# One stop for a unit's Gram products, its inverse in three parts of five steps, and fewer plain products between the mixers' steps

## The chip, the cores and the metric

The kernel runs on one core of a Trainium2 chip. The time is device microseconds from launch to end. It was 2159.46 us in the median of three runs (2154.07 to 2161.47).

## The reference

One transformer block over 1024 tokens of width 1024, in f32. Three stages add to the residual `x`:

```
x = x + 0.5 * (silu(norm(x) @ w_gate) * (norm(x) @ w_up)) @ w_down     # ffn 1, hidden 2816
proj = norm(x) @ w_in
o_gla  = gla(proj part)      # 4 heads, chunks of 64: decay, scores, state
o_rwkv = rwkv7(proj part)    # 8 heads of 64, token by token:
    sa    = state @ a_t
    state = state * w_t + sa b_t^T + v_t k_t^T
    y_t   = state @ r_t
x = x + concat(o_gla, o_rwkv) @ w_out
x = x + 0.5 * ffn 2(norm(x)) ; out = norm(x)
```

The token-by-token recurrence `rwkv7` is what the change is about. The kernel computes it in chunks of 64 tokens. Within a chunk, the effect of the tokens on one another is a triangular 64x64 system for each head. Its inverse is needed before the chunk's state can be taken on.

## The kernel before

**Halves.** The sequence is cut into two halves of 512 tokens, A and B. Every f32 product of the feed-forward parts and projections runs as three passes over operands split into a high and a low part (`mm3`). These are the *plain products* below: matmuls of 128x512, on TensorE one after the other. Their weights are staged by a cast on ScalarE (`wH`, L459) and a subtraction on VectorE (`wL`, L460), six buffers each.

**Mixers.** `mixers(h, filler, last)` runs once for A (with half B's ffn 1 as filler) and once for B (with half A's ffn 2 as filler). It has four streams:

- `Quad.prep` makes, for each of four units of two chunks (`u` = 0 to 3), the Gram products `pg` (L82 to L87), the 16x16 triangular inverse (L103 to L109: 15 steps of a shuffle, a multiplication and an addition on VectorE), then by small products `p1`, `p1b`, `p2`, `p2b` the 64x64 inverse, and `pav`.
- `Quad.loop` takes the state on, chunk by chunk: `pz`, `pu`, `px`, `py`, each waiting for an eviction of the one before.
- `Quad.norm` normalizes a unit's output: reductions and a Newton square root on VectorE (L226 to L233), four transposes `pyT`, eight scaled copies on ScalarE (L244), two operations on VectorE (L248), a store to DRAM (L249).
- `gla_unit`, twice: `pkv`, `pA`, five levels `pB`, `po`, `pt`.

**What sets TensorE's order.** Each stream yields a latency, `LAT[...]` times `SLACK` (1.49), in an estimated clock `T.ns` that adds up only TensorE's own work. As long as no stream is due, one plain product of the filler is put in. When some are due, those within `NEAR` take their next step, and then the filler gives `int(ns * FILL / 216 + 0.999)` plain products, `ns` being the estimate of what the steps took. TensorE keeps this order; the other engines' orders come from a list scheduler. That scheduler may also draw work from behind the mixers into places where it expects TensorE to be idle: the first `run(f1b, n=3)` after the mixers (two halves of a down product, one unit of gate and up: 96 plain products) lies among the mixers' steps.

**Behind the mixers.** `outprep` loads the mixers' results back from DRAM (`xnL`, L1289) and splits them (`xnH` on ScalarE, L1290; `xnL` on VectorE, L1291). They use memory that the mixers' tiles held. `outproj` multiplies them by `w_out` (`pout`), which needs the last unit's `norm` to have ended. For half B, `to_store(A)` also runs there: eight additions on GpSimd (`xs`, L717), each through one of the five buffers `t2` that the feed-forward's `silu` and `hf` use too, and a store each.

Of the kernel before, what the change touches and what calls it, by code (L numbers as in the profile page):

```python
# [5 lines left out]
CDEC=float(np.exp(-0.5))  # L6
MULT,ADD,SUB,MAX,MIN=ALU.mult,ALU.add,ALU.subtract,ALU.max,ALU.min

LAT=dict(pre=8000,gram=0,c32=3000,inv2=1400,D=900,m1=900,m2=900,x2=700,pav=900,w=600,z=1000,u=1000,x=1500,gn=6000,gpre=2635,gfirst=8000,lev0=5723,lev=1944,sc=770,on=8372)

def const_array():
    p=np.arange(128)
# [35 lines left out]
class Quad:  # L48
# [6 lines left out]
    def prep(self):  # L55
# [8 lines left out]
        for u in range(4):  # L64
# [8 lines left out]
            BK=BK.rearrange("p q (c r)->p q c r",c=2)  # L73
            yield LAT["pre"] if u==0 else 0

            WA=[mt([8,64],"WA","WA") for h in range(2)]
            W=st.W=[mt([8,64],"W","W") for h in range(2)]
            for i in range(2):
                c4=slice(4*i,4*i+4)
                pg=[ps(f"pg{h}").rearrange("p (e x t)->p e x t",e=4,x=2) for h in range(2)]  # L80
                for e in range(4):
                    q,c=2*i+e//2,e%2  # L82
                    for h in range(2):
                        T.matmul(pg[h][:,e],BK[fr[h],q,c],AR[fr[h],q,:,c,:],start=True,stop=True,tile_position=(64*h,0))
                for x,Wx in ((1,WA),(0,W)):
                    for h in range(2):
                        V.tensor_tensor(Wx[h][:,c4],pg[h][:,:,x],mg[:,x:x+1,:].to_broadcast([128,4,64]),op=MULT)  # L87
                yield LAT["gram"]

            c32=mt([8,32],"i2","c32")  # L90
            for h in range(2):
# [9 lines left out]
            V.tensor_copy(R16,C["i16"].rearrange("p (o t)->p o t",o=1).to_broadcast([128,8,16]))  # L101
            yield LAT["c32"]
            for j in range(15):  # L103
                n=15-j
                lb=mt([8,n],"lb","lb",bufs=2,padded_shape=[128,8,16])
                V.stream_shuffle(lb,c16[:,:,j+1:16],[j]*16+[16+j]*16)
                V.tensor_tensor(lb,lb,R16[:,:,j:j+1].to_broadcast([128,8,n]),op=MULT)
                V.tensor_tensor(R16[:,:,j+1:16],R16[:,:,j+1:16],lb,op=ADD)
                if j%2: yield LAT["inv2"]  # L109

            R=mt([8,32],"Rd","R")
            S.mul(R[:,:,0:16],R16,C["mq0"])
# [1 line left out]
            D=mt([8,32],"i2","D")  # L114
            V.transpose(D.rearrange("p c t->p (c t)"),R.rearrange("p c t->p (c t)"))
            yield LAT["D"]
            p1=ps("p1")[:,0:256].rearrange("p (c t)->p c t",t=32)
# [4 lines left out]
            S.copy(X1,p1)  # L122
            yield LAT["m1"]
            p1=ps("p1b")[:,0:128].rearrange("p (c t)->p c t",t=16)
# [4 lines left out]
            D=mt([8,32],"i2","D2")  # L129
# [29 lines left out]
            pav=ps("pav")  # L159
# [194 lines left out]
D = 1024  # L354
# [17 lines left out]
MUIDX = {**{f"r{i}": i for i in range(4)}, **{f"k{i}": 4 + i for i in range(4)}, **{f"v{i}": 8 + i for i in range(4)}, "wa": 12, "g": 13}  # L372
BUFS = dict(s2=7, W=4, WA=2, WN=4, AR=2, UV=2, AV=2, R64=2, s1=2, i2=3, g1=3, s3=2)
SLACK = 1.490
FILL = 0.549
PAHEAD = 2
NEAR = 254.150
NH, NL, NR = 6, 6, 4
# [14 lines left out]
def block_kernel(tc, ctx, x, consts, coff, vecs, finaln, wgu, wdn, win_t, win_v, w_out, alw, wa2, g2, out):  # L393
# [832 lines left out]
    def mixers(h, filler, last):  # L1226
# [40 lines left out]
        with tc.manual_schedule(engines={mybir.EngineType.PE}):  # L1267
            while True:
# [5 lines left out]
                if any(s.at <= t0 for s in can):  # L1274
                    for s in can:
                        if s.at <= T.ns + NEAR:
                            s.step()
                    n = int((T.ns - t0) * FILL / 216.0 + 0.999)
                for _ in range(n):
# [274 lines left out]
```

## Time and profile before

| | |
|---|---|
| profiled execution | 2156.78 us |
| its span, first to last instruction | 2155.0 us |
| median of three runs | 2159.46 us |
| TensorE (PE) busy | 2041.7 us, 95% |
| VectorE (DVE) busy | 1457.4 us, 68% |
| ScalarE (ACT), GpSimd (POOL) busy | 42%, 25% |
| mean granted clock of TensorE | 0.978 |

The profiled execution is 2.7 us under the median of the runs. A busy TensorE row counts pipelined matmuls, so 95% says only that TensorE is seldom idle. The useful question is where the remaining idle time lies and what ends it. The mixers of A run from 760 us, those of B from 1271 us.

### The profile page before, as it was taken

The page shows a single profiled execution, that of the slowest core. Times are in us where ns is not written, and L with a number is a line of the kernel's source. Part 1 is how long each engine was busy: PE and PEld are TensorE (multiplying, and loading weights), DVE is VectorE, ACT ScalarE, POOL GpSimd, SP SyncE. Part 2 cuts the span into 40 slices and gives each one's busy share as a digit, 9 for nine tenths or more (in the row PEclk, how much of TensorE's full clock was granted, in tenths as well). Part 3 has the DMA queues.
Part 4 walks back from the last instruction along what each step waited for, and adds up shares of the span by engine and source line. Part 5 has one row for each costly group of instructions (what it writes and reads, how often), then busy time and mean ns, then how long its engine had stood idle before and what let it go on. Part 6 is the DMA issues. An engine that isn't in the chain of part 4 may idle for free.

```text
span 2155.0 us, 36173 instructions
## 1 busy us (share of the span) xinstructions
PE 2041.7 (95%) x13516; PEld 1632.1 (76%) x13516; DVE 1457.4 (68%) x3043; ACT 909.9 (42%) x1699; POOL 549.3 (25%) x558
## 2 busy tenths in 40 slices
PE   8899999989999999996999999999598999998998
PEld 7777888867788877775788887777476788886886
DVE  6675778747739776775566956766577577874665
ACT  6432344322456545444365644534244243432143
POOL 0411555467012300000001310000112145647610
PEclk9999999999999999998999999999799999999999
DMA  5433344587355763333335683332433333448652
GB/s 192 128 117 112 124 146 166 205 312 270 131 177 187 234 187 110 114 104 134 126 124 181 215 260 123 115 109 80 161 130 106 112 127 132 161 167 341 244 171 74
DMA packets 172639, 345.20 MB, mean 160 GB/s; under 512 B 17296, under 2 KB 56240, under 8 KB 172464
## 3 DMA queue, kind: packets, MB, share of 16 engines
q1 hardware_dynamic: 145312, 251.13, 35.2%
q0 software_dynamic: 23552, 80.76, 10.4%
q10 hardware_dynamic: 3600, 11.01, 1.4%
q8 instruction: 106, 1.74, 0.3%
q14 instruction: 69, 0.57, 0.1%
HBM read 243.21 MB, written 99.61 MB: 159 GB/s over the span
## 4 chain that ended last, share of the span: by engine, by line
PE 81%; DVE 8%; DMA 4%; issue 2%; ACT 2%; POOL 2%; SPq 0%; ACTq 0%; DVEq 0%; POOLq 0%
PE pju L43 21%; PE pgu L43 17%; PE pp L43 11%; PE pdn L43 10%; PE pjd L43 7%; PE pout L43 4%; PE pv L43 2%; PE po L43 1%; PE py L43 1%; DVE wL L460 1%; DVE x L898 1%; DMA hh<-d_hid 1%; DVE T L696 1%; PE ptn L46 1%; PE pt L46 1%
## 5 line engine op out<-in xcount | busy, mean ns | idle before, releaser
L460 DVE TENSOR_TENSOR wL<-raw,wH 128x512 fp32r<-128x512 f32 (+1 forms) x382 | 274.2, 726 | 263.2 <-ACT wH L459 261.5
L459 ACT CAST wH<-raw 128x512 fp32r<-128x512 f32 (+1 forms) x382 | 233.6, 618 | 376.7 <-PE pgu L43 118.8
L43 PE MATMUL pgu<-xnH,wH 128*128 128x512 f32 (+1 forms) x656 | 259.4, 397 | 0.3 <-ACT xnH L518 0.2
L43 PE MATMUL pgu<-xnL,wH 128*128 128x512 f32 (+1 forms) x656 | 258.8, 396 | 0.0
L43 PE MATMUL pgu<-xnH,wL 128*128 128x512 f32 (+1 forms) x656 | 258.4, 395 | 0.0
L43 PE MATMUL pju<-T,wH 128*128 128x512 f32 x768 | 240.7, 394 | 2.4 <-ACT wH L695 2.4
L43 PE MATMUL pjd<-wH,hh 128*128 128x512 f32 x640 | 207.1, 403 | 13.1 <-DMA hh<-d_hid 12.7
L43 PEld LDWEIGHTS pju<-T,wH 128*128 128x128 f32 x768 | 144.3, 188 | 36.7 <-ACT wH L695 3.3
L43 PEld LDWEIGHTS pjd<-wH,hh 128*128 128x128 f32 x640 | 123.7, 193 | 45.0 <-issue 14.3
L43 PE MATMUL pju<-T,wL 128*128 128x512 f32 x384 | 151.4, 394 | 0.0
L43 PEld LDWEIGHTS pgu<-xnH,wH 128*128 128x128 f32 x656 | 124.7, 191 | 28.2 <-ACT xnH L518 1.1
L43 PEld LDWEIGHTS pgu<-xnL,wH 128*128 128x128 f32 x656 | 124.2, 190 | 27.6 <-DVE xnL L519 0.7
L43 PEld LDWEIGHTS pgu<-xnH,wL 128*128 128x128 f32 x656 | 124.0, 189 | 26.7 <-DVE wL L460 0.4
L43 PE MATMUL pdn<-wH,hH 128*128 128x512 f32 x320 | 129.9, 407 | 11.9 <-DVE hf L668 8.3
L43 PE MATMUL pp<-xnH,wH 128*128 128x512 f32 x352 | 140.7, 400 | 0.0
L43 PE MATMUL pp<-xnL,wH 128*128 128x512 f32 x352 | 138.9, 395 | 0.0
L43 PE MATMUL pp<-xnH,wL 128*128 128x512 f32 x352 | 138.9, 395 | 0.0
L43 PE MATMUL pjd<-wL,hh 128*128 128x512 f32 x320 | 129.6, 405 | 6.1 <-DVE wL L696 6.1
L43 PE MATMUL pdn<-wL,hH 128*128 128x512 f32 x320 | 129.3, 404 | 0.8 <-DVE wL L460 0.8
L43 PE MATMUL pdn<-wH,hL 128*128 128x512 f32 x320 | 129.0, 403 | 1.2 <-DVE hL L672 1.2
L696 DVE TENSOR_TENSOR wL<-s,wH 128x512 fp32r<-128x512 f32 x96 | 98.9, 1032 | 29.3 <-ACT wH L695 29.3
L631 DVE SCALAR_TENSOR_TENSOR x<-pdn,x 128x512 f32<-128x512 f32 x144 | 98.5, 686 | 28.9 <-PE pdn L43 27.8
(393 smaller groups left out, 4321.7 us busy)
## 6 DMA issues: line engine op xcount, KB each, us to landing
raw<-in_wgu_dram SPq DMA_DIRECT2D x256, 256.0 KB, 2.6
hh<-d_hid SPq DMA_DIRECT2D x80, 512.0 KB, 4.5
d_hid<-hh POOLq DMA_DIRECT2D x76, 512.0 KB, 3.7
raw<-in_win_t_dram SPq DMA_DIRECT2D x88, 256.0 KB, 3.1
raw<-in_wdn_dram SPq DMA_DIRECT2D x80, 256.0 KB, 2.8
wdk<-in_wdn_dram SPq DMA_DIRECT2D x24, 512.0 KB, 7.5
d_x<-x SPq DMA_DIRECT2D x20, 512.0 KB, 2.6
raw<-in_w_out_dram SPq DMA_DIRECT2D x32, 256.0 KB, 2.7
```

The source lines that it names most:

```text
L43: return self.t.matmul(out,lhsT,rhs,**kw)
L46: return self.t.transpose(out,in_,idn)
L459: S.copy(H, raw)
L460: V.tensor_tensor(L, raw, H.bitcast(F32), op=SUB)
L631: V.scalar_tensor_tensor(h.x[tt][:, co], ps, 0.5, h.x[tt][:, co], op0=MULT, op1=ADD)
L696: V.tensor_tensor(L, f, H.bitcast(F32), op=SUB)
L898: V.scalar_tensor_tensor(x, v, k, x, op0=MULT, op1=ADD)
```

## The change

Nothing is computed otherwise, and every engine has as many instructions of each kind as before (10892 matmuls, for one). What changes is where `prep` stops, with which latencies, and the filler's share.

```
-LAT=dict(pre=8000,gram=0,c32=3000,inv2=1400,D=900,m1=900,m2=900,...
+LAT=dict(pre=8000,gram=1500,c32=1600,inv5=3300,D=900,m1=900,m2=900,...
...
             for i in range(2):
                 ...                                  # 8 pg matmuls, 4 evictions L87
-                yield LAT["gram"]
+            yield LAT["gram"]
...
             for j in range(15):
                 ...                                  # shuffle, multiply, add
-                if j%2: yield LAT["inv2"]
+                if j%5==4: yield LAT["inv5"]
...
-FILL = 0.549
+FILL = 0.3
```

Both groups of Gram products now come at one stop. The inverse has three stops (after steps 5, 10 and 15) where it had seven. After a set of due steps the filler gives about half as many plain products.

TensorE, the end of half A's mixers, from the last state product `py` to the first product of `outproj`. Before:

```order
L43 MATMUL pz<-Xn,AR 64x64 x8
L43 MATMUL pgu<-xnL,wH 128x512
L43 MATMUL pgu<-xnH,wL 128x512
L43 MATMUL pu<-Z,R_9913 64x64 x8
L43 MATMUL px<-UV,WN 64x64 x8
L43 MATMUL py<-Xn,AR 64x64 x2
...
L43 MATMUL py<-UV,W 64x64 x2
L46 MATMUL pyT<-ct,AV 128x128 x4
L43 MATMUL pout_10345<-wH,xnH 128x512
```

And now:

```order
L43 MATMUL py<-UV,W 64x64 x2
L43 MATMUL pdn<-wH,hL 128x512
...
L43 MATMUL pdn<-wH,hL 128x512
L43 MATMUL pgu<-xnH,wH 128x512
...
L43 MATMUL pgu<-xnH,wL 128x512
L46 MATMUL pyT<-ct,AV 128x128 x4
L43 MATMUL pgu<-xnH,wH 128x512
...
L43 MATMUL pgu<-xnH,wL 128x512
L43 MATMUL pout_10345<-wH,xnH 128x512
```

40 `pdn` and 6 `pgu` stand between the last `py` and `pyT`, and 42 `pgu` between `pyT` and `pout`, where there was nothing. Of the 520 plain products that stood between the first `pg` and the last `py` of a mixer, 432 are left there. In half B it is the same.

ScalarE at the same place (`sq` is the square of L230, `wH` a cast of a weight). Before:

```order
L208 COPY AV<-py 128x256
L230 ACTIVATE sq_10092<-AV 128x512
L244 ACTIVATE AV<-pyT,vt 64x128 x8
L1290 CAST xnH<-xnL 128x512 x7
L459 CAST wH<-raw 128x512
```

And now:

```order
L208 COPY AV<-py 128x256
L230 ACTIVATE sq_10092<-AV 128x512
L459 CAST wH<-raw 128x512 x4
L244 ACTIVATE AV<-pyT,vt 64x128 x8
L459 CAST wH<-raw 128x512 x2
L665 ACTIVATE silu<-pgu 128x512
L459 CAST wH<-raw 128x512 x2
L1290 CAST xnH<-xnL 128x512
```

Eight casts of weights and one `silu` have come in between the last `py` and the first `xnH`, four casts and the `silu` of them behind L244.

VectorE there, in the middle of the Newton steps (`nwt`, `nwy`) of the last unit. Before:

```order
L231 TENSOR_REDUCE vr<-sq_10092 128x8
L485 TENSOR_SCALAR nwa<-vr 128x8
L486 TENSOR_SCALAR nwt<-nwa 128x8
L487 TENSOR_SCALAR nwy<-nwt 128x8
L492 TENSOR_TENSOR nwt<-nwy 128x8
L493 TENSOR_TENSOR nwt<-nwt,nwa 128x8
```

And now:

```order
L231 TENSOR_REDUCE vr<-sq_10092 128x8
L631 SCALAR_TENSOR_TENSOR x<-pdn,x 128x512
L485 TENSOR_SCALAR nwa<-vr 128x8
L460 TENSOR_TENSOR wL<-raw,wH 128x512
L486 TENSOR_SCALAR nwt<-nwa 128x8
L631 SCALAR_TENSOR_TENSOR x<-pdn,x 128x512
L487 TENSOR_SCALAR nwy<-nwt 128x8
L460 TENSOR_TENSOR wL<-raw,wH 128x512
L492 TENSOR_TENSOR nwt<-nwy 128x8
L631 SCALAR_TENSOR_TENSOR x<-pdn,x 128x512
L493 TENSOR_TENSOR nwt<-nwt,nwa 128x8
```

Evictions of the `pdn` products and subtractions of weights now stand among the steps of the norm; the last eviction but one stands ahead of the second Newton step's last operation (L494).

## Rows read from the trace of the kernel before

**Rows 1.** The page: busy time by engine, and TensorE in 40 slices

```profile
PE 2041.7 (95%) x13516; PEld 1632.1 (76%) x13516; DVE 1457.4 (68%) x3043; ACT 909.9 (42%) x1699; POOL 549.3 (25%) x558
...
PE   8899999989999999996999999999598999998998
```

**Rows 2.** TensorE's waits within half A's mixers: who, for whom, us, times, longest

```profile
PE pout L43 <- ACT xnH L1290: 9.5, 1, 9.5
PE pyT L46 <- DVE AV L233: 6.8, 1, 6.8
PE pA L43 <- DVE ke L289: 2.3, 2, 1.2
PE p2b L43 <- ACT X L141: 1.2, 2, 0.8
PE px L43 <- DVE UV L192: 1.1, 1, 1.1
```

**Rows 3.** The same within half B's mixers

```profile
PE pout L43 <- ACT xnH L1290: 11.4, 1, 11.4
PE pyT L46 <- DVE AV L233: 10.1, 1, 10.1
...
PE pu L43 <- DVE Z L186: 1.2, 1, 1.2
```

**Rows 4.** Timeline, end of half A's mixers: start us, us, engine, line, operation, tiles

```profile
995.34 0.42 DVE L201 TENSOR_TENSOR Xe<-Xt,pc 128x256 f32<-128x256 f32 x1
...
997.00 0.37 ACT L208 COPY AV<-py 128x256 f32<-128x256 f32 x1 [2.88 <-PE py L43]
...
1003.75 1.09 PE L46 MATMUL pyT<-ct,AV 128*128 128x128 f32 x4 [6.79 <-DVE AV L233]
1004.87 3.72 ACT L244 ACTIVATE AV<-pyT,vt 64x128 f32<-64x128 f32 x8 [5.14 <-PE pyT L46]
...
1009.35 0.69 DVE L248 TENSOR_TENSOR AV<-AV,g 128x512 f32<-128x512 f32 x1
...
1013.69 0.62 ACT L1290 CAST xnH<-xnL 128x512 fp32r<-128x512 f32 x1 [5.10 <-DMA xnL<-d_mix]
```

**Rows 5.** Timeline, end of half B's mixers: GpSimd beside VectorE

```profile
1509.13 1.59 POOL L717 TENSOR_TENSOR xs<-xnH,xnL 128x512 f32<-128x512 f32 x1 [37.40 <-ACT wH L459]
...
1511.64 2.92 DVE L201 TENSOR_TENSOR Xe<-Xt,pc 128x256 f32<-128x256 f32 x1
...
1515.19 2.65 DVE L227 TENSOR_SCALAR sm<-sm 128x8 f32<-128x8 f32 x1
1515.32 2.48 POOL L717 TENSOR_TENSOR xs<-xnH,xnL 128x512 f32<-128x512 f32 x2
```

**Rows 6.** The chain of waits in both halves: start us, us, what

```profile
962.40 7.65 PE pdn L43 x32
970.06 5.82 PE pgu L43 x25
...
1529.67 2.59 DMA d_mix<-AV
```

**Rows 7.** Stretches: us, busy by engine, granted clock of TensorE (PEclk), DMA

```profile
774.80:807.80 33.00, 31.92 (x502) 24.87 (x498) 30.39 (x121) 14.57 (x29) 0.20 (x1) 1.00 0.49 136
...
762.30:997.10 234.80, 228.95 (x3220) 175.26 (x3218) 165.89 (x593) 108.63 (x217) 1.77 (x5) 0.99 0.41 123
...
1014.30:1017.80 3.50, 3.44 (x8) 2.72 (x9) 2.56 (x4) 1.86 (x4) 0.00 (x0) 0.50 1.01 357
...
1390.80:1400.50 9.70, 9.70 (x33) 6.73 (x33) 1.98 (x3) 1.63 (x3) 0.00 (x0) 0.63 0.25 83
1400.50:1403.50 3.00, 3.00 (x8) 2.42 (x8) 1.95 (x6) 0.60 (x1) 0.00 (x0) 0.50 0.00 0
...
1535.80:1540.10 4.30, 4.30 (x10) 3.39 (x11) 2.92 (x5) 2.70 (x5) 0.00 (x0) 0.50 0.97 314
```

More of the change, by code (lines that the diff above doesn't have):

```diff
@@ L7 @@
 MULT,ADD,SUB,MAX,MIN=ALU.mult,ALU.add,ALU.subtract,ALU.max,ALU.min
-LAT=dict(pre=8000,gram=0,c32=3000,inv2=1400,D=900,m1=900,m2=900,x2=700,pav=900,w=600,z=1000,u=1000,x=1500,gn=6000,gpre=2635,gfirst=8000,lev0=5723,lev=1944,sc=770,on=8372)
+LAT=dict(pre=8000,gram=1500,c32=1600,inv5=3300,D=900,m1=900,m2=900,x2=700,pav=900,w=600,z=1000,u=1000,x=1500,gn=6000,gpre=2635,gfirst=8000,lev0=5723,lev=1944,sc=770,on=8372)
 def const_array():
```

## The prediction

> **What bounds the kernel now.** I read the page first. TensorE is busy 95% of the span, and no other engine over 68% [rows 1]; it has the same matmuls before and after. So a gain can only be idle time of TensorE that goes, or time in which it ran at half its clock. The slices show two dips, a 6 and a 5: the ends of the two mixers.
>
> The waits of each mixer then say what ended that idle time. In half A, 16.3 us lie in two waits: `pyT` waits 6.8 us for VectorE, and `pout` 9.5 us for ScalarE's `xnH`. All other waits listed there (`pA`, `p2b`, `px`) are 4.6 us [rows 2]. In half B the two are 10.1 and 11.4 us, together 21.5 [rows 3].
>
> The timeline shows what these waits are: a chain with no matmul in it. The last `py` is evicted at 997.0, the norm on VectorE runs until `pyT` at 1003.75, then come eight ScalarE copies (3.72 us), two VectorE operations until 1010.04, a store and a load, and a cast that starts at 1013.69 [rows 4]. The plain products that could have covered it had already been spent among earlier steps. After the chain TensorE's clock is at its lower level, 1.2 GHz (granted 0.50), for 3.5 us of `pout` in A and 4.3 us in B [rows 7], which had been preceded by these waits. At half speed, 3.5 and 4.3 us do the work of 1.8 and 2.1, so this costs 1.7 and 2.1 us.
>
> Chain and clock together: 16.3 + 1.7 = 18.0 us in A, 21.5 + 2.1 = 23.6 in B, 41.6 us in all.
>
> **The change, part by part.**
>
> *The filler's share.* This is the part that matters. 88 plain products move from among the steps to behind the last `py`: 46 ahead of `pyT`, 42 between `pyT` and `pout`. One plain product takes 7.65 / 32 = 0.239 or 5.82 / 25 = 0.233 us [rows 6]; I take 0.235. So 46 are 10.8 us, and 42 are 9.9.
>
> First wait: the norm needed 1003.75 - 997.0 = 6.75 us in A [rows 4]. In the changed order, evictions of `pdn` (L631) stand among its steps, and VectorE works in order. The last eviction that holds it back is that of the tile that ends with the 34th of the 40 `pdn`, 8.0 us behind `py`. Behind it come this eviction, four small operations, one `wL` and L233; with 0.69 us for one of 128x512, as L248 has [rows 4], and an estimated 0.2 for a small one, 3 x 0.69 + 0.8 = 2.9 us. `pyT` can start at 10.9 us, just when the 46 products end. I allow 0.3 us for each half. In B the 10.1 us held a collision besides: while GpSimd added for `to_store` (1.59 and 2.48 us), VectorE's L201 took 2.92 us, against 0.42 in A, and L227 took 2.65 [rows 4, 5]. These additions wait for buffers of the feed-forward's last unit, whose products now end only just ahead of `pout`; so the collision leaves this stretch.
>
> Second wait: from the start of `pyT` to that of the cast took 1013.69 - 1003.75 = 9.94 us, with 0.6 for the cast 10.6 [rows 4]. Now ScalarE casts two weights right behind L244, and VectorE's second L248 stands behind a subtraction that needs one of these casts: 0.6 + 0.6 us. SyncE issues one more weight load ahead of the `xnL` loads, about 0.3 us. That makes 12.1 us against 0.4 + 9.9 of TensorE's work, a rest of 1.7 us in A. In B the store has to land first (2.59 us [rows 6]); I estimate 2.3 us more there, a rest of 4.0. ScalarE also has two casts ahead of `xnH` whose buffers come free only when the 42 products end; 10.3 + 3 x 0.62 = 12.2 us, so these are as late as the chain and add nothing.
>
> The clock should then fall less. I keep a third of the 3.8 us, 1.3. In B, four of the GpSimd additions now run beside `pout`, at 1.24 us each as in the pairs of [rows 5], while VectorE splits `xnL`. TensorE needs 12 products (2.8 us) for each such piece, a pair blocks VectorE 2.5 us, so 1 us is lost. The Trainium skill (SBUF — State Buffer, "Who interferes with whom") states that VectorE with two SBUF inputs and GpSimd hold a shared port exclusively for a whole instruction. The trace agrees, with L201 at 2.92 us; by that rule the 5.0 us of additions could all be lost where they meet, 4 us more than my term.
>
> *Gram at one stop.* Eight matmuls and four evictions come a little earlier. Nothing waits for `pkv` behind them within the next 40 plain products (9.4 us). I cost it at nothing; without that cover it would be four evictions of some 0.4 us, 1.6 us for each unit.
>
> *The inverse in three parts.* The chain is the same. In unit 0 of each mixer its cover shrinks most. Between first Gram eviction and transposition, VectorE was busy 30.39 of 33.00 us [rows 7]: it was nearly the bound there. The changed order has 83 of its instructions in that stretch instead of 104. About ten of the 21 that leave are 128x512 (0.6 us each) and the others about 0.3, so 21 us busy and, with 2.6 idle as before, 24 us. TensorE now reaches `p1` after 67 plain products (15.7 us) and some 6 us of small steps, 22 us. So `p1` waits about 2 us, where it waited for nothing. In units 1 to 3 the stretch is longer than VectorE's work. Bounds for each mixer: no wait, or 33 - 22 = 11 us if VectorE's work there did not shrink at all.
>
> *Thinner cover at every step.* Few of some 70 small steps of a mixer are in the lists of waits; now most have 3 to 7 plain products (0.7 to 1.6 us) ahead of the next. The other waits listed are 2.3 + 1.2 + 1.1 = 4.6 us in A [rows 2], and in B `pu` waits 1.2 us besides such ones [rows 3]. I take these to come back the same, with unit 0's new 2 us balanced by waits that it overlaps with (`pA`, `p2b`). Bounds: all of them gone, 8 us better; or unit 0 at its far end in both mixers, some 18 us worse.
>
> The sum: 41.6 - (2 x 0.3 + 1.7 + 4.0) - 1.3 - 1.0 = 33.0 us. Against the profiled execution's 2156.8 that gives 2123.8; the median of the runs is 2.7 higher, and I take half of that: **2125 us**.
>
> **The rivals.**
>
> *The second wait stays.* The chain behind `pyT` gets as much longer as TensorE gets work, because ScalarE's casts and SyncE's loads for `w_out` queue ahead of it. For it: eight casts stand in between now. Against it: they take 5 us of ScalarE, half of them ahead of `pyT`. Then only the first waits go: 6.8 + 10.1 - 0.6 = 16 us, 2141.
>
> *The clock.* In B, the clock fell during one `po`: 9.7 us at 0.63 in the mean, then 3.0 at 0.50 [rows 7]. 0.63 means 7.2 us at the lower level, which with the 3.0 do the work of half that time: 5.1 us lost. Fewer plain products around small steps could make this happen at each of the four `po` (three more, 15 us): 2124 + 15, and a pair of shorter falls at 1.7 us each, 2142. Against it: the steps of A, two `po` among them, were granted 0.99 of the clock [rows 7]. The Trainium skill (TensorE: Matmul & The Clock Gate, "A second HAM failure mode") tells of a kernel in which TensorE's short idles between groups made the clock swing; the fall at the one `po` may be such a case, and A's steps show that such idles need not end so.
>
> *Slower: waits at the steps.* There are 140 small steps in all. If the thinner cover exposes their latency, each costs up to the 1.1 us that `px` waited with no plain product in front [rows 2]. 33 / 1.1 = 30 such waits eat the gain; from there the change is slower. With a third of the steps exposed (47) it is 2124 + 52 = 2176. Against it: `px` and `pu` are the shortest chains, and the changed order leaves 5 to 7 products in front of most of them.
>
> *That the change doesn't do what it says* is excluded by the order.
>
> **How the numbers follow.** My forecast 0.70 (2108 to 2136: all other waits and the rest of the second one gone, or unit 0 half way to its bound); the second wait stays 0.12 (2141); the clock 0.10 (2142); slower by waits 0.06 (2176); nothing gained 0.02. The range goes from 2108, which leaves little below, to 2147, which takes in the two middle rivals. A change under 0.3% (6.5 us) can't be told from none here: faster 0.88 (the first three cases, less 0.04 for what no row shows), within it 0.06 (nothing gained, and those 0.04), slower 0.06.
>
> **What would show it.** Right: in the changed profile no wait over 1 us of `pyT` for L233, a wait of `pout` of 1 to 5 us, the clock at 2.4 GHz when `pout` starts or shortly after, the two dips of TensorE's slices gone, and L201 in B at 0.42 us. Wrong: `pout` still waiting 9 us, granted clock of 0.5 in other stretches of the mixers, or many waits of `px`, `pu`, `p1` of about 1 us. A wait of `p1` in unit 0 well above 2 us would say that VectorE bounds the front of the mixers.

## The result and the profile after

The changed kernel takes 2131.28 us in the median (four runs, 2127.90 to 2133.31), against 2160.05 for the kernel before on the same chip: a ratio of 0.987, 95% interval 0.985 to 0.989. The profiled execution is 2131.11 us with a span of 2129.3 us, 25.7 less than before. The forecast was 2125.

The page, TensorE in 40 slices and the clock granted to it (answers to [rows 1]):

```profile
PE 2044.5 (96%) x13516; PEld 1633.4 (77%) x13516; DVE 1454.7 (68%) x3043; ACT 909.3 (43%) x1699; POOL 551.4 (26%) x558
...
PE   8999999989999999999999999999998999998998
...
PEclk9999999999999999999999999999998999999999
```

The two dips are gone. TensorE's waits in half A's mixers (us, times, longest; answers to [rows 2]):

```profile
PE p2b L43 <- ACT X L141: 3.7, 2, 2.0
PE pout L43 <- ACT xnH L1290: 3.3, 1, 3.3
PE pA L43 <- DVE ke L289: 1.8, 2, 1.3
PE pkv L43 <- DMA kN<-d_kN: 1.3, 1, 1.3
```

And in half B's ([rows 3]):

```profile
PE p2b L43 <- ACT X L141: 3.6, 2, 2.0
PE pout L43 <- ACT xnH L1290: 2.5, 1, 2.5
PE pA L43 <- DVE ke L289: 2.4, 2, 1.9
PE pkv L43 <- issue: 1.3, 1, 1.3
```

`pyT` no longer waits. `pout` waits 5.8 us in both halves together where it waited 20.9. A wait has grown that was 1.2 us in A and 0.8 in B: `p2b`, now 7.3 us in both together.

The timeline of A's tail (answers to [rows 4]; SPq is SyncE's DMA queue), in the answers for VectorE, TensorE, ScalarE and SyncE:

```profile
992.82 0.68 DVE L233 TENSOR_TENSOR AV<-AV,vr 128x512 f32<-128x512 f32 x1
...
993.65 0.63 PE L46 MATMUL pyT<-ct,AV 128*128 128x128 f32 x4
...
982.74 0.37 ACT L208 COPY AV<-py 128x256 f32<-128x256 f32 x1 [3.83 <-PE py L43]
...
994.31 3.73 ACT L244 ACTIVATE AV<-pyT,vt 64x128 f32<-64x128 f32 x8 [1.43 <-PE pyT L46]
...
1006.73 0.62 ACT L1290 CAST xnH<-xnL 128x512 fp32r<-128x512 f32 x1 [2.21 <-DMA xnL<-d_mix]
...
1000.05 0.57 SPq L249 DMA_DIRECT2D d_mix<-AV  x1
1000.72 0.57 SPq L452 DMA_DIRECT2D raw<-in_w_out_dram  x1
1001.37 5.00 SPq L1289 DMA_DIRECT2D xnL<-d_mix  x8
```

The norm now ends 10.8 us behind the eviction at 982.74 instead of 6.75, and TensorE gets there at the same moment. From `pyT` to the first cast it is 13.1 us (before: 9.9), of which TensorE fills 9.9.

Where the 25.7 us come from, worked out from the starts and ends of TensorE's rows. The first column is the time from the end of the projection to the end of the last `py`. The second leads from there to the start of the last of the four `pyT`, the third on to the start of the first `pout`:

| us | A: to last `py` | to `pyT` | to `pout` | B: to last `py` | to `pyT` | to `pout` |
|---|---|---|---|---|---|---|
| before | 236.6 | 7.5 | 9.9 | 241.5 | 10.8 | 11.8 |
| changed | 221.2 | 11.3 | 13.4 | 222.6 | 11.2 | 12.5 |

88 products (20.7 us) went from the first column to the others. The tails grew by 7.3 and 1.1 us only, so they saved 13.4 + 19.6 = 33.0. The first columns should have shrunk by 20.7 each and shrank by 15.4 and 18.9: 7.1 us were given back there. 33.0 - 7.1 = 25.9. These 7.1 us are a net figure. In the profile before, the clock had fallen for 10.2 us at B's `po` (5.1 us lost, [rows 7]), and in the changed one it does not fall there; without this the steps gave back 12.2 us.

### The profile page after: what moved, and what is told of

It reads as the page before. It is cut to its first block, busy times and chain, and to the rows that moved or that the text cites. A ratio compares the mean times of both kernels' runs of the same rounds, so it can differ in the third digit from the quotient of the medians.

```text
span 2129.3 us, 36214 instructions
## 1 busy us (share of the span) xinstructions
PE 2044.5 (96%) x13516; PEld 1633.4 (77%) x13516; DVE 1454.7 (68%) x3043; ACT 909.3 (43%) x1699; POOL 551.4 (26%) x558
## 4 chain that ended last, share of the span: by engine, by line
PE 81%; DVE 7%; DMA 6%; ACT 3%; issue 2%; POOL 1%; SPq 0%; ACTq 0%; DVEq 0%
PE pju L43 21%; PE pgu L43 16%; PE pp L43 12%; PE pdn L43 10%; PE pjd L43 6%; PE pout L43 4%; PE pv L43 2%; PE py L43 2%; DMA hh<-d_hid 1%; PE po L43 1%; DVE x L898 1%; DVE wL L460 1%; DVE T L696 1%; DMA xw<-d_xf 1%; PE pt L46 1%
## 5 line engine op out<-in xcount | busy, mean ns | idle before, releaser
L43 PEld LDWEIGHTS pjd<-wH,hh 128*128 128x128 f32 x640 | 125.0, 195 | 47.3 <-issue 16.8
L43 PE MATMUL pdn<-wH,hH 128*128 128x512 f32 x320 | 132.2, 414 | 11.3 <-DVE hf L668 7.7
```

The lines of the kernel that those rows point to most:

```text
L43: return self.t.matmul(out,lhsT,rhs,**kw)
```

## The experiments

Ratios are against the kernel before on the same chip, with 95% intervals; times are medians. The runs come from several chips, and the kernel before took 2156.0 to 2160.1 us there in the median, so a difference between the times of two runs is uncertain by some 4 us.

**1, 2. Each part alone.** FILL alone (`FILL = 0.3`, stops and LAT of before), and the new stops and LAT alone (`FILL = 0.549`).

> The kernel before with the new FILL alone: stops and LAT of before, 54 plain products behind the last py (34 ahead of pyT, 20 between pyT and pout) instead of none; the changed kernel has 46 and 42. Theory one (the gain is the cover that these products give to the two waits of each mixer's tail): 34 x 0.235 = 8.0 us takes pyT's waits from 6.8 and 10.1 to 0 and about 2, 20 x 0.235 = 4.7 us takes pout's from 9.5 and 11.4 to about 5 and 7; some 24 us of idle time go, a few come back as waits at the mixers' steps: 2138, ratio 0.990. Rival (the gain comes from the new stops of Gram products and inverse): 2158, ratio 0.999, with the tail's idle time given back at the steps.

> The changed kernel with the FILL of before: new stops and LAT, 58 plain products behind the last py (37 and 21). Theory one: like the run with FILL alone in the tail (some 24 us of idle time go), less some 7 us that the changed kernel lost in the waits of p2b behind ScalarE's L244 if these come from the stops: 2141, ratio 0.991. Rival (the gain comes from the stops): 2133, ratio 0.987, as much as the whole change. If the waits of p2b are there with the old FILL too, they come from the stops; if not, from the thinner fill.

Measured: FILL alone 2151.1, ratio 0.997 (0.995 to 0.999); stops alone 2147.7, ratio 0.995 (0.993 to 0.996). Both expectations missed: the two parts alone bring 0.3% and 0.5%, together 1.3%. From TensorE's waits over the whole run, with FILL alone and then with the stops alone:

```profile
PE pout L43 <- ACT xnH L1290: 17.4, 2, 9.1
...
PE p L43 <- DVE D L115: 7.9, 4, 2.1
```

```profile
PE pout L43 <- ACT xnH L1290: 17.5, 2, 9.4
...
PE pyT L46 <- DVE AV L233: 11.8, 4, 4.1
...
PE p2b L43 <- ACT X L141: 2.7, 3, 1.2
```

In the tail both did a good part of what theory one says. With 34 and 37 products ahead of `pyT` its wait there goes (the 11.8 us of the second run lie at the `pyT` of earlier units). `pout`'s 20.9 us only shrink to 17.4 and 17.5, where theory one had some 12. By the starts and ends of TensorE's rows the two tails still won 21.0 and 21.2 us, near the 24 expected. But the time to the last `py` went down by only 2.9 and 11.3 us in the first run and 4.0 and 9.4 in the second, where 54 and 58 products fewer would have made 12.7 and 13.6. With the old stops and the small FILL, `p` waits for VectorE's inverse; with the new stops and the old FILL, the `pyT` of an earlier unit comes up before its norm is ready. The clock fell behind such waits too: in A's steps 6.8 us were lost to it with FILL alone and 8.5 with the stops alone (two falls behind waits, and one at a `po`), against 1.7 in the kernel before. Each part is paid for by waits at the steps that the other part avoids.

**3. The copy of `p2`'s result on VectorE.** The changed kernel with

```
-                S.copy(X2[rb],p2[rb])
+                V.tensor_copy(X2[rb],p2[rb])
```

The reason is in the changed kernel's timeline, ScalarE and TensorE at one `p2b` of half A (L133 and L134 multiply for the 64x64 inverse, L141 is the copy):

```profile
909.83 3.72 ACT L244 ACTIVATE AV<-pyT,vt 64x128 f32<-64x128 f32 x8 [2.80 <-DVE R L128]
913.58 0.51 ACT L133 ACTIVATE R<-R,ct 128x256 f32<-128x256 f32 x1
914.00 0.49 ACT L134 ACTIVATE R<-R,ct 128x256 f32<-128x256 f32 x1
914.51 0.75 ACT L141 COPY X<-p 32x256 f32<-32x256 f32 x2
...
914.93 1.08 PE L43 MATMUL p2b<-R,X 32*32 32x32 f32 x32 [1.99 <-ACT X L141]
```

In the new order the `pyT` of the unit before stands between `p1b` and `p2` in the last two units of each mixer, so its eight copies of 3.72 us, and two more multiplications, are ahead of the small copy that `p2b` waits for.

> The changed kernel with the two copies of p2's result (L141) on VectorE instead of ScalarE; the order of TensorE's instructions stays. Theory two (p2b waits since the copy stands behind the eight multiplications of L244 on ScalarE, 3.7 us, and TensorE's clock falls behind the waits): p2b's 7.3 us go, with up to three stretches of half clock at 1.7 us each: 2122, from 2119 to 2125. Rival (VectorE is as late: the copies take their place in a queue that is busy 21 of 23 us at the inverse, and other waits grow as much): 2131, as the changed kernel.

Measured: 2120.0, ratio 0.982 (0.980 to 0.984), 11.3 us under the changed kernel. The waits in half A are then these:

```profile
PE pout L43 <- ACT xnH L1290: 3.3, 1, 3.3
PE pA L43 <- DVE ke L289: 2.5, 2, 2.0
PE pkv L43 <- DMA kN<-d_kN: 1.4, 1, 1.4
```

`p2b` is gone, in B too. The clock goes with it. Stretches of the changed kernel at half clock (us, busy by engine, then the granted clock; answers to [rows 7]):

```profile
790.30:793.70 3.40, 3.40 (x14) 2.73 (x9) 3.17 (x18) 1.66 (x7) 0.00 (x0) 0.50 0.00 0
916.60:920.00 3.40, 3.40 (x30) 2.46 (x30) 1.90 (x3) 2.09 (x4) 0.00 (x0) 0.50 0.38 102
961.00:964.40 3.40, 3.40 (x36) 2.56 (x35) 0.69 (x1) 0.66 (x2) 0.00 (x0) 0.50 0.27 78
1008.80:1012.20 3.40, 3.40 (x10) 2.62 (x9) 2.28 (x4) 1.57 (x4) 0.00 (x0) 0.50 0.96 355
1292.10:1295.50 3.40, 3.40 (x70) 2.85 (x60) 3.40 (x16) 1.55 (x6) 0.00 (x0) 0.50 0.05 15
1418.40:1425.20 6.80, 6.70 (x72) 5.26 (x73) 2.67 (x5) 3.04 (x7) 0.00 (x0) 0.50 0.27 78
1510.50:1513.90 3.40, 3.40 (x10) 2.62 (x9) 3.04 (x4) 1.43 (x4) 3.02 (x3) 0.50 0.91 255
```

Three of these follow `p2b` waits (916.60, which begins 1.7 us behind that of 914.93, 961.00 and 1418.40); they lose half of 13.6 us, 6.8. Two follow waits of `pA` (790.30 and 1292.10, 3.4 us lost), and two stand at `pout`. With X2 on VectorE the three behind `p2b` are gone, and one at another place has come (1.7). 7.3 us of waits and 5.1 of clock make 12.4, near the 11.3 measured. The times to the last `py` are now 216.5 and 216.1: 20.1 and 25.4 under those of before, the first about what 88 products make, the second that and the 5.1 us of `po`.

**4. The same in the kernel before**, with its own order.

> The kernel before with X2 on VectorE and nothing else. Theory two says that the wait behind ScalarE's L244 is of the changed kernel's order, in which pyT of the unit before stands between p1b and p2: here p2b waits only 2.0 us in all, so 2158, ratio 0.999, from 2154 to 2160. Rival (the copy on ScalarE is slow in any order): some 11 us less, as in the changed kernel, 2149.

Measured: 2158.1, ratio 0.999 (0.997 to 1.002). So in the old order the copy on ScalarE costs nothing that can be told from none, as theory two says.

**5. The products held back.** The changed kernel with the filler stopped as soon as only `norm` is left, and the rest issued behind `outproj`:

```
+                if all(s.gen is norm_ for s in todo):
+                    filling = False
...
-    run(f1b, n=3)
-    outproj(A)
-    run(f1b)
+    with tc.manual_schedule(engines={mybir.EngineType.PE}):
+        outproj(A)
+        run(f1b)
...                                                   # for B in the same way
```

> The changed kernel with the plain products behind each mixer's last steps (96 a mixer: 46 ahead of pyT, 42 between pyT and pout, 8 among the last pu and px) held back until the output projection of that mixer has run; everything ahead of them stays. Theory one (the products do nothing but cover the two tail waits): both waits come back, some 7 and 10 us in A and 7 and 10 in B, with 2 us of half clock each and 1 to 2 us at the last steps: 34 to 42 us more than the changed kernel, 2169, slower than the kernel before. Rival (the gain comes from the stops of the Gram products and the inverse, and the tail's idle time is given back in another place): less than 15 us more, 2131 to 2146.

Measured: 2160.2, ratio 1.000 (0.998 to 1.002): nothing of the change's gain is left. TensorE's waits for the two in the whole run:

```profile
PE pout L43 <- ACT xnH L1293: 20.8, 2, 11.1
PE pyT L46 <- DVE AV L233: 15.9, 2, 9.1
```

Both waits are back at the size of before. The rise of 28.9 us is under the expected 34 to 42, since the held products also cover other work behind `pout`: from its end to the next stage it took 63.1 and 144.4 us, 20.3 and 14.8 more than in the changed kernel, for 22.6 us of products each. The `manual_schedule` block also fixes TensorE's order behind `pout`, which the list scheduler set before.

**6. More and fewer products.** The changed kernel with `FILL = 0.15` and with `FILL = 0.42`.

> The changed kernel with FILL 0.15: 118 products behind the last py of each mixer (41 ahead of pyT, 77 between pyT and pout) instead of 88. Theory one, now with its price (each product taken from between the steps leaves up to 0.235 us of wait there): pout's waits of 3.3 and 2.6 us and the half clock behind them (3.4) go, 9 us, while 30 products fewer between the steps, 7.1 us a mixer, come back in part as waits: 2131, from 2124 to 2140, so no gain over the changed kernel. Rival (the more behind the mixer the better): 2122.

> The changed kernel with FILL 0.42: 71 products behind the last py (40 and 31) instead of 88. Theory one: the 11 products fewer between pyT and pout cost 2.6 us in each mixer as longer pout waits, and the steps, which lost some 5 us of waits in each mixer, get 17 products more and win about as much: 2133, from 2127 to 2140. Rival (the gain grows with the products behind py alone): 17 x 2 x 0.235 = 8 us are lost, 2139.

Measured: 2130.5, ratio 0.985 (0.983 to 0.988), for 0.15; 2136.7, ratio 0.989 (0.987 to 0.992), for 0.42. The first came as theory one priced it. The second lies in its range, but between its 2133 and the rival's 2139: `pout` waits 11.5 us instead of 5.9, as expected, but the steps won nothing. Their 17 products more are 4.0 us, and the times to the last `py` grew by 5.8 and 4.2. With 0.15 `pout` waits for nothing, but the granted clock fell at the small products of unit 0 (a stretch of A, columns as above):

```profile
801.60:815.30 13.70, 12.79 (x301) 9.81 (x301) 6.10 (x14) 5.32 (x11) 0.00 (x0) 0.50 0.21 60
```

That is 6.8 us lost, and 10.2 in each mixer with the other such stretches (5.1 in the changed kernel), and `pA` waits 9.5 us instead of 4.2.

**7. What is left of `pout`'s wait.** X2 on VectorE, and four of the eight loads that `pout` needs issued by GpSimd, since those tiles come from the other mixer:

```
-            nc.sync.dma_start(raw, ...
+            (nc.gpsimd if kt < 4 else nc.sync).dma_start(raw, ...
```

> The run with X2 on VectorE, and the loads of xnL for tiles 0 to 3 (L1289) issued by GpSimd instead of by SP, where they stand behind the last store of d_mix and behind loads of w_out; those four tiles come from the other mixer, which is long done. Theory three (the rest of pout's wait is the queue that xnL's loads stand in, not the data): pout waits 0 instead of 3.3 and 2.6, and the half clock behind them (3.4 us) goes: 2120 less 9, 2111, from 2109 to 2115. Rival (the wait is the landing of the last store and the memory of the mixer that comes free late, or w_out's loads, which share the DMA engines): 2120, as with X2 alone.

Measured: 2125.4, ratio 0.983 (0.981 to 0.986): no gain, and `pout` waits 9.4 us. This did not test the theory. At unit 0's small products in A the clock also fell for 13.7 us behind a wait of `pB`, where it had not with X2 alone. The four loads of A were issued at 926.8 to 928.9, but ScalarE's queue had tile 4's cast ahead of tile 0's, and that waited for its own load:

```profile
998.31 0.62 ACT L459 CAST wH<-raw 128x512 fp32r<-128x512 f32 x1 [2.17 <-PE pgu L43]
1001.14 4.26 ACT L1290 CAST xnH<-xnL 128x512 fp32r<-128x512 f32 x8 [2.21 <-DMA xnL<-d_mix]
```

So it was run again with the casts of tiles 4 to 7 kept behind the others:

```
+                with tc.issue_after(i1.ins) if kt > 3 else nullcontext(), ...
```

> As the run with X2 on VectorE and the loads of xnL's tiles 0 to 3 from GpSimd (which landed some 70 us ahead), but with the casts of tiles 4 to 7 kept behind those of tiles 0 to 3 on ScalarE; in the run before, tile 4's cast was queued first and waited for its load until 1001.1. Theory three (the rest of pout's wait is the queue and not the data): tile 0 is cast at about 999, right behind the last weight cast, pout starts some 2 us sooner in A and as much or nearly so in B, the half clock behind the wait may go (1.7 us each): 2116, from 2112 to 2119, against 2120 with X2 alone. Rival (pout is held by something else, as w_out's casts or the landing of the last tiles, and GpSimd's queue only disturbs): 2120 to 2126.

Measured: 2120.1, ratio 0.984 (0.982 to 0.985), the same as with X2 alone. The halves differ. In A the cast comes right behind the weight cast, and `pout` waits 1.0 us instead of 3.3; its block of 192 matmuls takes 44.8 us instead of 46.3, with no fall of the clock. In B GpSimd's loads stood waiting until the last store had landed, and `pout` waits 5.2 us instead of 2.6; its block takes 49.3 us instead of 46.3. ScalarE in A, GpSimd in B:

```profile
996.02 0.61 ACT L1293 CAST xnH<-xnL 128x512 fp32r<-128x512 f32 x1
```

```profile
1488.95 2.18 POOL L1291 DMA_DIRECT2D xnL<-d_mix  x4 [71.94 <-DMA d_mix<-AV]
```

Theory three holds in A; in B the edit made the wait that it was to remove, so it stays untested there.

**8. The collision in B.** The kernel before with `outproj(B)` ahead of `to_store(A)` in the program.

> The kernel before with the eight additions of GpSimd for the store of A (L717) issued behind the output projection of B instead of ahead of it; TensorE's order stays. If their collision with VectorE's L201 and L227 (2.92 and 2.65 us where A has 0.4) makes B's first tail wait longer than A's, pyT's wait in B falls from 10.1 to about 7, as in A: 2157. Rival: the collision is hidden or the additions then fall on something else that is late: 2160, no change. Either way most of the 17.8 us that the change gained in B is the products' cover and not the collision.

Measured: 2158.3, ratio 1.000 (0.998 to 1.002). It says nothing: the list scheduler left GpSimd's additions beside the norm (from 1503.08), and L201 took as long. What the collision alone costs stays open. L201 at B's tail, shortest, median and longest in ns:

```profile
L201 DVE TENSOR_TENSOR Xe<-Xt,pc x1: 2920/2920/2920, 1505.6 to 1505.6; 128x256 f32<-128x256 f32 x1
```

**9. Both repairs together: a better version.** The changed kernel with X2 on VectorE and `FILL = 0.22`, and with `FILL = 0.22` alone.

> The changed kernel with X2 on VectorE and FILL 0.22: 121 products behind the last py (41 and 80) instead of 88. The run with FILL 0.15 and X2 on ScalarE took as long as the changed kernel: it won pout's 5.9 us and 3.4 us of half clock and lost as much in waits at the steps. If that loss is the thin fill itself, this run is like X2 alone: 2120, from 2116 to 2125. Rival (the loss there was ScalarE's queue at p2b again): pout's waits go and nothing comes back, 2112.

> The changed kernel with FILL 0.22 and X2 on ScalarE as before; TensorE's order is that of the run with FILL 0.22 and X2 on VectorE (2111.5). pyT stands ahead of p2 or p2b in three units of each mixer again, so if the waits behind L244 are worth what they were at FILL 0.3 (11 us), this is 2122, from 2117 to 2126, and both parts add: FILL 0.22 gives some 9 us by itself and 0.15 was too thin. Rival (the copy's engine matters only at FILL 0.3, and FILL 0.22 alone is the better version): 2112.

Measured: both together 2111.5, ratio 0.980 (0.979 to 0.982), 19.7 us under the changed kernel; FILL alone 2121.2, ratio 0.983 (0.980 to 0.985). The two repairs bring 11.3 and 10.1 us apart and 19.7 together; by the ratios it is 10.8, 9.5 and 14.7, so it is not shown that both add in full. With both, these are the waits in A's mixers that are over 1 us:

```profile
PE pB L43 <- issue: 2.7, 2, 1.5
PE pA L43 <- DVE ke L289: 1.9, 2, 1.3
```

`pout` waits in neither half, and its blocks take 44.7 and 44.6 us, 1.6 less than in the changed kernel. The clock does not fall there, as a stretch of A's `pout` shows, from 3.5 us behind its first product on:

```profile
997.40:1001.00 3.60, 3.60 (x17) 2.93 (x16) 0.44 (x1) 1.06 (x2) 0.00 (x0) 1.00 0.85 321
```

The clock still falls at other places, for 20.5 us in both mixers together, and 10.2 are lost. The rival of the first of these runs had the time right (2112): at 0.22 the thin fill costs little, and it was 0.15 that cost. Its reason, ScalarE's queue at `p2b`, does not hold: with 0.15 `p2b` waits for nothing. With FILL 0.22 alone, `p2b` waits 3.6 us in all; what makes the rest of the 9.7 us between the two runs stays open, since its profile is of its longest execution (2130.4).

## Why the prediction was right

The time, 2131, is 6 us above the forecast and inside its range and its main case. Step by step:

- **What bounds the kernel**: right, and shown. With the products held back (5.) the two waits come back and the whole gain goes.
- **First wait**: 0.3 us for each half, measured none. The norm was reckoned to end 10.9 us behind `py`, and ended 10.8.
- **Second wait**: 1.7 + 4.0 = 5.7 us, measured 3.3 + 2.5. The sum is right by luck, of two errors that cancel. In A I had put 0.3 us on SyncE's extra load; the eight issues took 5.00 us (4.19 before), and from issue to landing it was 5.8 us in the median, against 4.2 before. In B I had added 2.3 us for the store's landing, of which no more than 0.8 showed.
- **Clock behind it**: 1.3 us kept, measured 3.4. Waits of 3.3 and 2.5 us still left TensorE at 1.2 GHz for 3.4 us in each half; the fall did not come where `pout` waited 1.0 us or not at all (FILL 0.15 in 6., A in the second run of 7., both together in 9.: blocks of 44.6 to 44.8 us).
- **GpSimd beside `pout`**: VectorE's split (L1291) took up to 2.45 us there, against 0.69 alone. By the Trainium skill (SBUF — State Buffer, "Who interferes with whom") a VectorE instruction with two SBUF inputs contends with a GpSimd instruction that reads SBUF; the trace agrees. But B's block of `pout` takes 46.3 us as A's does, where no additions run: it cost 0, not 1.0 or 4. And L201 took 0.88 us in B (2.92 before [rows 5]), not 0.42: two additions still ran there, from 1480.87 and 1483.54.
- **Gram at one stop**: put at 0; `pkv` now waits 1.3 us in each half, in A for a load and so not for Gram evictions, in B with nothing listed, so the cause there is open.
- **Inverse in three parts**: 24 us in unit 0 with 21 busy, measured 23.0 and 21.2. `p1` waited for nothing; I had 2 us.
- **Thinner cover at the steps**: this is the term that was mis-sized. I had waits and savings cancel; measured 7.1 us lost, or 12.2 without the 5.1 us of B's `po`. Of the 12.2, 3.7 are waits: those listed at the steps of both mixers went from 13.1 to 16.8 us, `p2b`'s alone from 2.0 to 7.3. The other 8.5 are the clock, whose falls cost 10.2 us there, and 1.7 before apart from `po`. The 2 us that I had `pA` and `p2b` absorb were looked for on VectorE. Most of the cost comes from ScalarE: moving `pyT` in between `p1b` and `p2` put L244 ahead of L141. I had followed L244 in the tail and not in the units before it. The X2 run wins 11.3 us.

By these terms the sum of 33.0 us becomes 33.0 - 7.1 (steps) - 2.1 (clock) + 1.0 (GpSimd) + 0.5 (waits) = 25.3; the spans differ by 25.7.

Of the rivals, the second wait did not stay (5.8 of 20.9 us). The clock rival had the right mechanism at the wrong place: it fell behind `p2b` and `pA`, not at `po`, and cost 10.2 us in the steps and not 15 more. So one of the signs that I had set down for being wrong did come, a granted clock of 0.5 in other stretches of the mixers. The fall at `po` is no fixed cost of the order. TensorE's order is the same in the kernel before and in the runs of 4. and 8. At the `po` of the second `gla_unit` the clock fell for 10.2 us in B only in the profile of the first, in both halves in that of the second, and in neither in that of the third, behind waits of 0.57 to 0.61 us each time. B's `po` in 4. and then in 8. (columns as above):

```profile
1398.90:1409.10 10.20, 10.20 (x28) 7.28 (x29) 2.77 (x8) 1.19 (x2) 0.00 (x0) 0.50 0.20 69
```

```profile
1385.00:1400.00 15.00, 14.39 (x126) 10.35 (x124) 7.68 (x24) 6.08 (x13) 0.00 (x0) 1.00 0.36 118
```

So the 5.1 us by which B gained there are not shown to be the change's.

The slower rival did not come in the changed kernel, but 1. and 2. show its mechanism: with either part alone, the steps give back 11.2 and 13.8 us of the 21 that the tails win.

## What to carry over

A wait at the end of a stage can be closed with work taken from earlier in the stage, but count what the thinned steps give back: the two parts of this change were worth 7 and 10 us alone and 29 together. When a change of order moves a step, follow what that step queues on the in-order engines at every place where it lands, not only at the one that is being repaired; 3.7 us of copies in front of a 0.4 us one cost 11 us here, where the change gained 29. And look at what one engine's queue puts in front of a load or cast whose data are long there, before blaming the transfer; in 7. a new order of loads and casts cut `pout`'s wait in A from 3.3 to 1.0 us, though a longer wait in B took the gain back.

## What was not expected of the hardware

- The granted clock of TensorE fell to 1.2 GHz behind single waits. In the changed kernel it fell for 3.4 or 6.8 us behind waits of `pA` (1.31 and 1.88), `p2b` (1.99, 1.71 and 2.00) and `pout` (3.34 and 2.51), the last two with 42 full matmuls ahead of the wait. Behind `p2b`'s fourth wait (1.60) and `pkv`'s two (1.26 and 1.30) it did not fall, and with no wait at `p2b` or `pout` it stayed at 2.4 GHz there.
- At one `po` it fell for 10.2 us in some profiles and not at all in others, with TensorE's order and the wait ahead of it (0.57 to 0.61 us) the same.
- It fell for 13.7 us at the small products of unit 0 with FILL 0.15 (TensorE busy 12.79 us), behind a wait of `pB` of 2.25 us, and with FILL 0.3 in the first run of 7., behind one of 1.60.
- Eight loads of 256 KB landed 5.8 us after issue (median) where one more load of 256 KB was issued just ahead of them, as in the changed kernel, and 5.5 us with FILL alone, which has that load too; in the kernel before, without it, they took 4.2. That this load is the cause was not tested.
